# Seven products of quarters instead of eight in the first product of both swiglus

## The chip, the cores and the metric

The kernel runs on one core of a Trainium2 chip. Five compute engines with queues of their own work side by side: PE multiplies matrices into PSUM, ACT, DVE and POOL work on elements, SP starts transfers. The metric is the device time of one launch in microseconds (us). A profiled execution adds a trace; all times of single instructions below are from that one.

## The reference, cut to what matters

Two transformer blocks of D = 1024 are computed one after the other, all in fp32. The first has two layers over 512 latent tokens (and, in layer 0, 256 context tokens), each a mixer and then a swiglu of hidden width 2816:

```
def swiglu(h, w_in, w_out):
    gt, up = jnp.split(h @ w_in, 2, axis=-1)
    return (jax.nn.silu(gt) * up) @ w_out
...
hf = rms_norm(x, norm_ffn[l]) * (1.0 + sc_f) + sh_f
x = x + g_f * swiglu(hf, ffn_w_in[l], ffn_w_out[l])
```

In layer 0 the swiglu runs over 512 + 256 = 768 tokens, in layer 1 over 512. The second block (two layers, another kind of MLP) is not touched by the change.

## The kernel before, in words

Activations lie transposed: features on the 128 partitions, 8 slices k of 128 features, tokens along the free dimension (`XT` latent, `XC` context). An fp32 product is made of three faster ones: a factor is split into a rounded high part and the rest (`split`: a cast on ACT, a subtraction on DVE), and high x high, high x low and low x high are added up in PSUM (`product`, L273, L275, L277).

Weights come through the class `Weights`: SP loads a block of up to 2048 columns into a buffer `wst` (`WST` = 2 of them and the block in use), ACT casts it to `whi` (L91), DVE subtracts to `wlo` (L92), each with `WSP` = 2 buffers. So a block is split while the one before is multiplied, and its cast waits until PE has left the buffer two blocks back.

`swiglu` goes over the hidden width in 22 tiles of 128 rows. One tile (`up`) is one weight block of two products, gate and up (8 slices x 3 matmuls each, over 512 + 258 columns in layer 0 and 256 + 258 in layer 1; two columns carry the shift `sh_f`). DVE takes each from PSUM: L648 copies the shift columns, L649 multiplies by `rb`, the row of 1/rms; then ACT makes Silu (L651), DVE the product with the up part (L652), and `split` makes `uh` and `ul`. After 8, 7 and 7 tiles the second product (`down`) runs over what is there, in four steps of two output tiles, and adds its share to the residual (L450). The last part's `down` steps also feed the next norm.

The input of the first product is formed by `feed_mod(k)` as each slice k of the residual is finished: POOL adds its square to `acc` (L328, for the norm), ACT scales and casts it to `nmh` (L597), DVE makes `nml` (L598). The factor 1/rms is not known then; it is applied after the product, by `rb`, which is made within the first tile (`rstd`, L418, and `rbcast`, L343).

The program is written in steps; within an engine the order of instructions is set by a scheduler, each engine then runs its own queue in order and waits at its head. PSUM is handed out in four tiles of 1024 columns (`ps()`).

Of the kernel before, what the change touches and what calls it, by code (L numbers as in the profile page):

```python
# [23 lines left out]
WST = 2  # L24
WSP = 2
# [31 lines left out]
class Weights:  # L57
# [21 lines left out]
    def split(self, i):  # L79
        b = self.b  # L80
        nc = b.nc
        stage, n = self.loaded[i]
        self.loaded[i] = None
        desc, raw = self.desc[i]
        if raw:
# [3 lines left out]
        hi = b.wpool.tile([P, 2048], FR, tag="whi", name="whi", bufs=WSP)  # L89
        lo = b.wpool.tile([P, 2048], FR, tag="wlo", name="wlo", bufs=WSP)  # L90
# [29 lines left out]
class Builder:  # L120
# [158 lines left out]
    def pair(self, tiles, xh, xl, k0=0, kt=KT, outs=None, first=True, last=True):  # L279

        ps = self.ps() if outs is None else outs
        self.product(
            tiles, xh, xl, k0, kt, [(0, L)], [[ps[:, j * L : (j + 1) * L]] for j in range(len(tiles))], first, last
        )
        return ps

# [292 lines left out]
    def open_mod(self, l, side):  # L579


        n = L if l else T
        self.enter("nm", nm=(1, None, side))
        parts = [self.nm.tile([P, KT, n + 32], FR, name=m) for m in ("nmh", "nml")]
        self.feeds = parts + [self.nm.tile([P, n], F32, name="nmr"), self.nm.tile([P, KT, 4], F32, name="nmg")[:, :, 0:2]]
        self.gains(l, 1, self.feeds[3])
        self.split(self.M[:, l, 24:32, :], *(a[:, :, n : n + 2] for a in parts))

    def feed_mod(self, k, n):

        nc = self.nc
        hi, lo, _, G = self.feeds
        for z, (c0, m) in enumerate([(0, L)] + ([(L, C)] if n > L else [])):
            self.squares(k, c0, m, nc.gpsimd)
            g = G[:, k, z : z + 1]
            h = hi[:, k, c0 : c0 + m]
            nc.scalar.activation(h, self.x(k, c0, m), AF.Copy, scale=g)  # L597
            nc.vector.scalar_tensor_tensor(  # L598
                lo[:, k, c0 : c0 + m], self.x(k, c0, m), g, h.bitcast(F32), ALU.mult, ALU.subtract
            )  # L600


    def swiglu(self, l):
        wi, wo = self.I["ffn_w_in"][l], self.I["ffn_w_out"][l]
        n = T if l == 0 else L
        if l == 1:
            self.step(lambda: self.open_norm(("norm_mix_2", 0)))
        self.scope_step("ffn", hid=(1, None))

        if n == T:  # L610
            segs, at = [(0, L), (L, C + 2)], [(0, L), (L, T + 2)]
            tokens = lambda a: a[:, 0:T]
            runs = [(lambda a: a[:, 0:L], T), (lambda a: a[:, L:T], T + 1)]
        else:
            segs, at = [(0, C), (C, C + 2)], [(0, C), (L, L + C + 2)]
            tokens = lambda a: a.rearrange("p (s n) -> p s n", n=a.shape[1] // 2)[:, :, 0:C]
            runs = [(tokens, L + C)]

        def product(tile):
            o = self.ps()  # L620
            hi, lo, _, _ = self.feeds
            self.product([tile], hi, lo, 0, KT, segs, [[o[:, a:e] for a, e in at]])
            return o

        parts = [(0, 8), (8, 7), (15, 7)]
        for q, (t0, nt) in enumerate(parts):

            def alloc():
                self.uh = self.hid.tile([P, 8, n], FR, tag="uh", name="uh")
                self.ul = self.hid.tile([P, 8, n], FR, tag="ul", name="ul")  # L630

            self.step(alloc)
            for i in range(nt):

                def up(v, i=i, start=q == 0 and i == 0):
                    nc = self.nc
                    rb = self.feeds[2]
                    og = product(v[0])
                    if start:
                        self.rstd(n)  # L640
                    ou = product(v[1])
                    if start:
                        nc.scalar.copy(rb, self.rbcast(n)[:, 0:n])
                    s, u = self.t(n), self.t(n)
                    sh = self.tmp.tile([P, 2, 2], F32, tag="sh", name="sh")
                    c = runs[0][1]
                    for y, o, d in ((0, og, s), (1, ou, u)):
                        nc.vector.tensor_copy(sh[:, y], o[:, c : c + 2])  # L648
                        nc.vector.tensor_tensor(tokens(d), tokens(o), tokens(rb), ALU.mult)  # L649
                    for z, (run, _) in enumerate(runs):  # L650
                        nc.scalar.activation(run(s), run(s), AF.Silu, bias=sh[:, 0, z : z + 1])  # L651
                        nc.vector.scalar_tensor_tensor(run(s), run(u), sh[:, 1, z : z + 1], run(s), ALU.add, ALU.mult)  # L652
                    self.split(s, self.uh[:, i, :], self.ul[:, i, :])

                self.step(up, (blk(wi, 0, KT, (t0 + i) * P, P), blk(wi, 0, KT, FF + (t0 + i) * P, P)))
            for i in range(0, KT, 2):

                def down(v, i=i, q=q, nt=nt):
                    if n == T:
                        outs = self.full(cols(v), self.uh, self.ul, 0, nt)  # L660
                    else:
                        o = self.pair(cols(v), self.uh, self.ul, 0, nt)
                        outs = [o[:, 0:L], o[:, L : 2 * L]]
                    for j in range(2):
                        k = i + j
                        self.residual(outs[j][:, 0:L], k, 0, L, self.mod(l, 5, k, 0))
                        if n == T:
                            self.residual(outs[j][:, L:T], k, L, C, self.mod(l, 5, k, 1))
                        if q == 2:
                            if n == T:  # L670
                                self.squares(k, 0, L)
                                self.squares(k, L, C)
                            else:
                                self.feed(k)

                self.step(down, (blk(wo, t0, nt, i * P, 2 * P),))
        self.leave_step("ffn")
        self.leave_step("nm")
# [169 lines left out]
def even_mixer(b):  # L848
# [1491 lines left out]
```

## Time and the profile before

| | |
|---|---|
| median of 3 runs | 3628.89 us (3626.35 to 3630.6) |
| profiled execution, its time | 3626.45 us |
| its span (first to last instruction) | 3624.4 us |
| mean granted TensorE clock | 0.988 of full speed |
| busy: PE, DVE, ACT, POOL | 96%, 50%, 33%, 2% of the span |

The span is all but 2 us of the time. A busy share is an average over stages: what an engine can take on in one stage is read from that stage's rows. An instruction's time in a row runs from its start to its end, and neighbours overlap at their edges by some 0.08 us.

### The profile page before, as it was taken

To read this page: it belongs to the slowest core of one execution; us is meant where nothing else is said; L and a number is where in the kernel's file an instruction comes from. 1 tells how busy PE (TensorE), PEld (TensorE's weight loads), DVE (VectorE), ACT (ScalarE), POOL (GpSimd) and SP (SyncE) were. 2 spreads that over 40 slices of the span, in tenths; PEclk is the share of its full clock that TensorE was granted. 3 is DMA by queue.
4 is the path that set the end of the run, shared out by engine and by line. 5 is a ranking of instruction groups with operands and counts; after the bars stand their busy time and mean duration, and the time that the engine had idled before them with its cause. 6 is when DMAs were issued, how large, how long until landed. Compare 5 with 4: busy or idle time off the path is not lost.

```text
span 3624.4 us, 46788 instructions
## 1 busy us (share of the span) xinstructions
PE 3495.5 (96%) x19754; PEld 3013.2 (83%) x19754; DVE 1807.6 (50%) x3145; ACT 1187.7 (33%) x1810; POOL 72.0 (2%) x87
## 2 busy tenths in 40 slices
PE   6999899999999989999999999999999999999998
PEld 4767777888888879988999888888889999988886
DVE  5657555653233345565444555444554444454445
ACT  4356545432121233343222322222334234222222
POOL 0000000020000001001000000000000000000000
PEclk9999999999999999999999999999999999999999
DMA  6111455422222223222333233333232222233332
GB/s 232 48 57 65 147 165 190 138 59 70 59 64 59 66 85 82 74 63 82 94 89 100 85 88 106 98 99 93 87 102 77 83 71 76 75 95 93 93 98 71
DMA packets 351873, 333.17 MB, mean 92 GB/s; under 512 B 22192, under 2 KB 293296, under 8 KB 351664
## 3 DMA queue, kind: packets, MB, share of 16 engines
q1 hardware_dynamic: 330320, 313.88, 27.8%
q10 hardware_dynamic: 21344, 16.30, 1.5%
q8 instruction: 155, 2.54, 0.3%
q14 instruction: 54, 0.44, 0.0%
HBM read 312.62 MB, written 15.96 MB: 91 GB/s over the span
## 4 chain that ended last, share of the span: by engine, by line
PE 91%; DVE 4%; ACT 2%; DMA 1%; issue 1%; SPq 0%; POOL 0%; ACTq 0%; DVEq 0%
PE ps L277 19%; PE ps L275 19%; PE ps L273 19%; PE ps L310 5%; PE ps L312 5%; PE ps L311 5%; PE ps L1332 3%; PE ps L1704 1%; PE ps L1705 1%; PE ps L1706 1%; PE psc L1332 1%; PE ds L986 1%; PE pp L273 1%; PE pp L275 1%; PE pa L515 1%
## 5 line engine op out<-in xcount | busy, mean ns | idle before, releaser
L91 ACT CAST whi<-wst 128x2048 fp32r<-128x2048 f32 (+5 forms) x245 | 442.1, 1805 | 1281.5 <-PE ps L275 910.9
L92 DVE TENSOR_TENSOR wlo<-wst,whi 128x2048 fp32r<-128x2048 f32 (+5 forms) x245 | 529.8, 2162 | 157.3 <-ACT whi L91 150.2
L275 PE MATMUL ps<-ul,whi 128*128 128x512 f32 (+1 forms) x1040 | 361.9, 375 | 0.0
L277 PE MATMUL ps<-uh,wlo 128*128 128x512 f32 (+1 forms) x1040 | 361.4, 375 | 0.0
L273 PE MATMUL ps<-uh,whi 128*128 128x512 f32 (+1 forms) x1040 | 359.8, 374 | 0.0
L277 PE MATMUL ps<-nhh,wlo 128*128 128x512 f32 x864 | 340.1, 394 | 0.0
L275 PE MATMUL ps<-nhl,whi 128*128 128x512 f32 x864 | 338.0, 392 | 0.0
L273 PE MATMUL ps<-nhh,whi 128*128 128x512 f32 x864 | 337.0, 390 | 0.0
L275 PE MATMUL ps<-nml,whi 128*128 128x258 f32 (+2 forms) x1408 | 322.7, 310 | 2.3 <-DVE nml L598 2.0
L273 PE MATMUL ps<-nmh,whi 128*128 128x258 f32 (+2 forms) x1408 | 319.9, 309 | 4.2 <-ACT nmh L597 4.2
L277 PE MATMUL ps<-nmh,wlo 128*128 128x258 f32 (+2 forms) x1408 | 322.5, 310 | 0.6 <-DVE wlo L92 0.6
L310 PE MATMUL ps<-whi,nhh 128*128 128x512 f32 x576 | 238.0, 413 | 0.0
L273 PEld LDWEIGHTS ps<-nmh,whi 128*128 128x128 f32 x1408 | 216.8, 188 | 20.8 <-issue 4.6
L275 PEld LDWEIGHTS ps<-nml,whi 128*128 128x128 f32 x1408 | 216.4, 189 | 18.4 <-DVE nml L598 4.1
L277 PEld LDWEIGHTS ps<-nmh,wlo 128*128 128x128 f32 x1408 | 216.7, 189 | 16.2 <-DVE wlo L92 0.9
L311 PE MATMUL ps<-wlo,nhh 128*128 128x512 f32 x576 | 230.2, 400 | 0.0
L312 PE MATMUL ps<-whi,nhl 128*128 128x512 f32 x576 | 229.9, 399 | 0.0
L275 PEld LDWEIGHTS ps<-ul,whi 128*128 128x128 f32 x1040 | 184.1, 188 | 38.3
L273 PEld LDWEIGHTS ps<-uh,whi 128*128 128x128 f32 x1040 | 183.0, 188 | 36.6
L277 PEld LDWEIGHTS ps<-uh,wlo 128*128 128x128 f32 x1040 | 183.6, 188 | 35.5
L275 PEld LDWEIGHTS ps<-nhl,whi 128*128 128x128 f32 x864 | 162.2, 188 | 37.5
L273 PEld LDWEIGHTS ps<-nhh,whi 128*128 128x128 f32 x864 | 162.2, 188 | 35.4
(439 smaller groups left out, 6037.1 us busy)
## 6 DMA issues: line engine op xcount, KB each, us to landing
wst<-in_ffn_w_in_dram SPq DMA_DIRECT2D x88, 512.0 KB, 4.9
wst<-in_ada_w_dram SPq DMA_DIRECT2D x42, 1024.0 KB, 5.2
wst<-in_attn_w_qkv_dram SPq DMA_DIRECT2D x36, 1024.0 KB, 5.1
wst<-in_mlp_w_up_dram SPq DMA_DIRECT2D x32, 1024.0 KB, 5.5
wst<-in_mlp_w_down_dram SPq DMA_DIRECT2D x32, 1024.0 KB, 5.0
wst<-in_even_w_in_dram SPq DMA_DIRECT2D x14, 1024.0 KB, 5.3
wst<-in_ffn_w_out_dram SPq DMA_DIRECT2D x16, 896.0 KB, 4.6
wst<-in_odd_w_in_dram SPq DMA_DIRECT2D x12, 1024.0 KB, 5.2
```

The costliest lines, as they stand in the source:

```text
L91: nc.scalar.copy(hi[:, :n], stage[:, :n])
L92: nc.vector.tensor_tensor(lo[:, :n], stage[:, :n], hi.bitcast(F32)[:, :n], ALU.subtract)
L273: nc.tensor.matmul(outs[t][s], wh[:, k, :], xh[:, k0 + k, c0 : c0 + n], start=st, stop=False)
L275: nc.tensor.matmul(outs[t][s], wh[:, k, :], xl[:, k0 + k, c0 : c0 + n], start=False, stop=False)
L277: nc.tensor.matmul(outs[t][s], wl[:, k, :], xh[:, k0 + k, c0 : c0 + n], start=False, stop=sp)
L310: nc.tensor.matmul(o, lhs_h(4 * kk + k, 2 * i + j), wh[:, k, :], start=st, stop=False)
L311: nc.tensor.matmul(o, lhs_h(4 * kk + k, 2 * i + j), wl[:, k, :], start=False, stop=False)
L312: nc.tensor.matmul(o, lhs_l(4 * kk + k, 2 * i + j), wh[:, k, :], start=False, stop=sp)
L515: nc.tensor.matmul(ps[32 * k : 32 * k + 32, :], self.c2[:, a + 32 * k : a + 32 * k + 32], v[:, k, :], start=st, stop=sp,)
L986: nc.tensor.matmul(ps[:, o : o + w_], b.qkT[0][rows, h, j * P : (j + 1) * P], b.qkT[1][rows, h, c0 : c0 + w_], start=True, stop=True,)
L1332: mark = nc.tensor.matmul(out, lhsT, rhs, start=start, stop=stop)
L1704: nc.tensor.matmul(o, b.hh[:, k, at], wh[:, k, :], start=k == 0, stop=False)
```

## The change: what it does

The weight of a tile is a 2 x 2 matrix of quarters: rows gate (a11, a12) and up (a21, a22), columns the first and the last four slices k. The input is cut likewise: b11 and b12 are the two halves of the tokens for k < 4, b21 and b22 for k >= 4. The product of 2 x 2 quarters, eight products of quarters before, is made as seven (Strassen's algorithm in Winograd's form): P1 = a11 b11, P2 = a12 b21, P3 = s1 t1, P4 = s2 t2, P5 = s4 b22, P6 = s3 t3, P7 = a22 t4, where the s are sums of weight quarters and the t sums of input quarters. Each is 4 slices x 3 matmuls over 384 + 2 columns in layer 0 and 256 + 2 in layer 1: 84 matmuls for a tile.

`combine` forms the weight sums on POOL (L123 in the numbering of the changed kernel; ring `ws` of `WSUM` = 5), and splits in two groups, {a11, a12, s1, s2} and {s4, s3, a22}: six casts and six subtractions of 3584 columns in all, where there was one of each over 2048. Each group takes one `whi` and one `wlo` buffer. `quarters` runs the products in PSUM areas R, Q and V and takes them out between: ACT copies R or V to SBUF, DVE adds Q, V or R to the copies. The multiplication by `rb` is no longer part of the eviction: it follows on SBUF data, on DVE for gate and on POOL for up (L780).

`feed_mod` forms and splits b11, t1 (k < 4) and b21, b22, t2 (k >= 4) with each slice. `rest_mod` forms t3 (POOL) and t4 (DVE) within the first tile, after P3. `down` runs after 4, 4, 4, 4, 4 and 2 tiles, in two steps of four output tiles, so residuals are added six times. In the mixer of layer 0 the slices are fed in another order.

```diff
+        if raw == FAST:
+            self.done.append(self.combine(stage, desc))
...
+    def combine(self, stage, desc):
...
+            nc.gpsimd.tensor_tensor(s, a, b, op)
...
+        s1 = sum_(a21, a22, ALU.add)
+        s2 = sum_(s1, a11, ALU.subtract)
+        s4 = sum_(a12, s2, ALU.subtract)
+        s3 = sum_(a11, a21, ALU.subtract)
+        out = {}
+        for group in (((("a11", "a12"), v[:, 0]), (("s1",), s1), (("s2",), s2)), ((("s4",), s4), (("s3",), s3), (("a22",), a22))):
+            hi, lo = (t.rearrange("p (i k c) -> p i k c", i=4, c=P)[:, :, :q] for t in self.parts())
...
+                self.b.split(src, h, l)
...
+    def quarters(self, w, x, n, g, u, late=None):
...
+        add(R, "a11", "b11", True)
+        nc.scalar.copy(g[:, 0], R)
+        add(Q, "a12", "b21", True)
+        add(V, "s1", "t1", True)
+        nc.scalar.copy(u[:, 1], V)
+        nc.vector.tensor_tensor(g[:, 0], g[:, 0], Q, ALU.add)
+        if late is not None:
+            late()
+        add(R, "s2", "t2", False)
+        nc.scalar.copy(g[:, 1], R)
+        add(V, "s4", "b22", False)
+        nc.vector.tensor_tensor(g[:, 1], g[:, 1], V, ALU.add)
+        add(R, "s3", "t3", False)
+        nc.scalar.copy(u[:, 0], R)
+        nc.vector.tensor_tensor(u[:, 1], u[:, 1], R, ALU.add)
+        add(Q, "a22", "t4", True)
+        nc.vector.tensor_tensor(u[:, 0], u[:, 0], Q, ALU.add)
...
+            nc.vector.tensor_tensor(t2, t2h, t2l, ALU.add)
+            nc.gpsimd.tensor_tensor(t3, t2, b11h, ALU.subtract)
+            nc.gpsimd.tensor_tensor(t3, t3, b11l, ALU.subtract)
+            nc.vector.tensor_tensor(t4, b21h, t2, ALU.subtract)
+            nc.vector.tensor_tensor(t4, t4, b21l, ALU.add)
+            self.factor("t3", k, t3)
+            self.factor("t4", k, t4)
...
-        parts = [(0, 8), (8, 7), (15, 7)]
+        parts = [(t0, min(4, FF // P - t0)) for t0 in range(0, FF // P, 4)]
...
+                    for d, eng in ((s, nc.vector), (u, nc.gpsimd)):
+                        eng.tensor_tensor(d[:, :, 0:m], d[:, :, 0:m], rb, ALU.mult)
```

How the queues change is shown at three places of layer 1. On ACT, two tiles in the middle of the first part of 8 stood like this before (L651 Silu, L91 the next block's cast, L242 `uh`):

```order
L651 ACTIVATE t_15115<-t_15115,sh_15117 128x512 [waits DVE_49]
L91 CAST whi_15129<-wst_15008 128x2048 [waits DMAHW1_49,DMAHW2_49,PE_49,Activation_49]
L242 CAST uh_15015<-t_15115 128x512 [waits DVE_49]
L651 ACTIVATE t_15231<-t_15231,sh_15233 128x512 [waits DVE_49]
L91 CAST whi_15245<-wst_15126 128x2048 [waits DMAHW3_49,DMAHW4_49,PE_49,Activation_49]
L242 CAST uh_15015<-t_15231 128x512 [waits DVE_49]
```

In the changed kernel one tile in the middle of a part has these rows (t_16605 and t_16606 are the gate and up buffers of this tile, t_16474 the gate buffer of the tile before, whi_16589 the first group of the tile after; L348, L351, L356 and L360 are the copies after P1, P3, P4 and P6):

```order
L348 COPY t_16605<-ps_16607 128x258 [waits PE_49]
L283 CAST uh_16472<-t_16474 128x512 [waits DVE_49]
L351 COPY t_16606<-ps_16608 128x258 [waits PE_49]
L283 CAST whi_16589<-wst_16445 128x1024 [waits DMAHW3_49,PE_49,Activation_49]
L283 CAST whi_16589<-ws_16581 128x512 [waits Pool_49]
L283 CAST whi_16589<-ws_16583 128x512 [waits Pool_49]
L356 COPY t_16605<-ps_16607 128x258 [waits PE_49]
L360 COPY t_16606<-ps_16607 128x258 [waits PE_49]
L784 ACTIVATE t_16605<-t_16605 128x256 [waits DVE_49]
L784 ACTIVATE t_16605<-t_16605 128x256
L283 CAST whi_16597<-ws_16585 128x512 [waits PE_49,Activation_49,Pool_49]
```

ACT now holds copies that PE waits for, and the copy after P4 stands behind three casts for the next tile; the cast of `uh` stands between the copies of the next tile.

On POOL nothing stood there before. Now, at the same place (wst_16445 is the block of the third tile of the part, wst_16578 that of the fourth; t_16475 and t_16606 are the up buffers of the first and the second):

```order
L123 TENSOR_TENSOR ws_16581<-wst_16445 128x512 [waits DMAHW4_49,DVE_49]
L123 TENSOR_TENSOR ws_16583<-ws_16581,wst_16445 128x512 [waits DMAHW3_49,DVE_49,Pool_49]
L123 TENSOR_TENSOR ws_16585<-wst_16445,ws_16583 128x512 [waits DVE_49,Pool_49]
L780 TENSOR_TENSOR t_16475<-t_16475,nmr_14256 128x2x256 [waits DVE_49]
L123 TENSOR_TENSOR ws_16587<-wst_16445 128x512 [waits DVE_49]
L123 TENSOR_TENSOR ws_16711<-wst_16578 128x512 [waits DMAHW6_49,DVE_49]
L123 TENSOR_TENSOR ws_16713<-ws_16711,wst_16578 128x512 [waits DMAHW5_49,DVE_49,Pool_49]
L123 TENSOR_TENSOR ws_16715<-wst_16578,ws_16713 128x512 [waits DVE_49,Pool_49]
L780 TENSOR_TENSOR t_16606<-t_16606,nmr_14256 128x2x256 [waits DVE_49]
```

The multiplication that a tile's up half waits for stands behind three weight sums of a tile two further on.

On DVE, where layer 1's first tile begins, these rows stood before (L450 the last residuals of the mixer, L598 the last three `nml`):

```order
L450 SCALAR_TENSOR_TENSOR XT_70<-ps_13784,M_90,XT_70 128x512 [waits PE_49]
L450 SCALAR_TENSOR_TENSOR XT_70<-ps_13784,M_90,XT_70 128x512
L92 TENSOR_TENSOR wlo_13813<-wst_13692,whi_13812 128x2048 [waits DMAHW4_49,DMAHW3_49,Activation_49]
L598 SCALAR_TENSOR_TENSOR nml_13704<-XT_70,nmg_13706,nmh_13703 128x512 [waits DVE_49,Activation_49] x3
L648 COPY sh_13959<-ps_13835 128x2 [waits PE_49]
```

Now 27 rows stand between the last residual and the last low part of t3; the last of them (L716 the low parts of b21 and b22, L737, L740 and L741 the sums for t3 and t4, ps_14479 an area of the first tile, wlo_14429 the low part of the second tile's first group):

```order
L716 SCALAR_TENSOR_TENSOR b21l_14251<-XT_70,nmg_14257,b21h_14250 128x256 [waits Activation_49]
L716 SCALAR_TENSOR_TENSOR b22l_14253<-XT_70,nmg_14257,b22h_14252 128x256 [waits Activation_49]
L284 TENSOR_TENSOR t2l_14255<-t_14413,t2h_14254 128x256 [waits Activation_49]
L737 TENSOR_TENSOR scr_14472<-t2h_14254,t2l_14255 128x256 x2
L740 TENSOR_TENSOR scr_14472<-b21h_14250,scr_14472 128x256 [waits DVE_49] x2
...
L352 TENSOR_TENSOR t_14476<-t_14476,ps_14479 128x258 [waits Activation_49]
...
L284 TENSOR_TENSOR wlo_14429<-wst_14215,whi_14428 128x1024 [waits DMAHW3_49,PE_49,Activation_49]
L284 TENSOR_TENSOR wlo_14429<-ws_14420,whi_14428 128x512 [waits Activation_49]
L284 TENSOR_TENSOR wlo_14429<-ws_14422,whi_14428 128x512 [waits Activation_49]
L284 TENSOR_TENSOR t4l_14464<-scr_14472,t4h_14463 128x256 [waits Activation_49]
L284 TENSOR_TENSOR t3l_14462<-scr_14473,t3h_14461 128x256 [waits Activation_49]
```

The last low part of t3 stands behind a weight group whose cast waits for the end of P4 of the same tile.

## Rows read from the trace of the kernel before

**Rows 1.** The page: busy time by engine, and the chain that ended last.
```profile
PE 3495.5 (96%) x19754; PEld 3013.2 (83%) x19754; DVE 1807.6 (50%) x3145; ACT 1187.7 (33%) x1810; POOL 72.0 (2%) x87
...
PE 91%; DVE 4%; ACT 2%; DMA 1%; issue 1%; SPq 0%; POOL 0%; ACTq 0%; DVEq 0%
```

**Rows 2.** Timeline, DVE, layer 0's swiglu: start, us, instruction, idle before and its releaser.
```profile
1004.04 0.16 DVE L648 COPY sh<-ps 128x2 f32<-128x2 f32 x1 [3.05 <-PE ps L277]
...
1020.84 0.16 DVE L648 COPY sh<-ps 128x2 f32<-128x2 f32 x1 [3.05 <-PE ps L277]
```

**Rows 3.** Timeline, DVE, layer 1's swiglu.
```profile
1833.24 0.16 DVE L648 COPY sh<-ps 128x2 f32<-128x2 f32 x1 [4.91 <-PE ps L277]
...
1844.58 0.16 DVE L648 COPY sh<-ps 128x2 f32<-128x2 f32 x1 [4.91 <-PE ps L277]
```

**Rows 4.** Groups of ACT by line and shape: count | busy us, mean ns | idle before.
```profile
L242 ACT CAST uh<-t 128x512 fp32r<-128x512 f32 x22 | 13.7, 622 | 2.7 <-DVE t L652 2.1
L91 ACT CAST whi<-wst 128x1024 fp32r<-128x1024 f32 x9 | 9.5, 1053 | 44.1 <-PE ps L275 38.4 <-issue 5.6
L1506 ACT COPY vv<-ps 128x384 f32<-128x384 f32 x32 | 15.2, 478 | 18.1 <-PE ps L1332 17.8
L1112 ACT COPY XC<-pp 128x256 f32<-128x256 f32 x12 | 4.4, 370 | 4.4 <-PE pp L277 4.4
```

**Rows 5.** Groups of DVE by line and shape.
```profile
L243 DVE TENSOR_TENSOR ul<-t,uh 128x768 fp32r<-128x768 f32 x22 | 20.9, 951 | 0.9 <-ACT uh L242 0.9
L652 DVE SCALAR_TENSOR_TENSOR t<-t,sh 128x512 f32<-128x512 f32 x44 | 33.1, 752 | 4.5
L598 DVE SCALAR_TENSOR_TENSOR nml<-XT,nmg,nmh 128x512 fp32r<-128x512 f32 x16 | 18.4, 1163 | 0.9 <-ACT nmh L597 0.9
L243 DVE TENSOR_TENSOR ul<-t,uh 128x512 fp32r<-128x512 f32 x22 | 15.1, 684 | 0.1
L92 DVE TENSOR_TENSOR wlo<-wst,whi 128x1024 fp32r<-128x1024 f32 x9 | 11.0, 1223 | 2.7 <-ACT whi L91 2.2
L328 DVE TENSOR_TENSOR acc<-acc,t 128x256 f32<-128x256 f32 x16 | 6.8, 423 | 8.3 <-ACT t L327 7.7
```

**Rows 6.** Groups of POOL by line and shape.
```profile
L328 POOL TENSOR_TENSOR acc<-acc,t 128x512 f32<-128x512 f32 x14 | 24.5, 1751 | 548.2 <-PE ps L277 365.2 <-ACT t L327 182.7
L1689 POOL TENSOR_TENSOR B<-al,fconsts 128x512 f32<-128x512 f32 x12 | 15.8, 1346 | 120.5 <-DVE z L1782 58.1 <-DVE z L1779 36.6 <-DMA al<-in_rpbr_dram 16.9
L376 POOL TENSOR_TENSOR hl<-t,hh 128x768 fp32r<-128x768 f32 x8 | 14.7, 1834 | 579.9 <-PE pa L515 561.8 <-DVE t L374 18.1
```

**Rows 7.** Timeline, POOL, where layer 1's swiglu begins.
```profile
1681.93 6.26 POOL L328 TENSOR_TENSOR acc<-acc,t 128x512 f32<-128x512 f32 x3 [1.58 <-ACT t L327]
```

**Rows 8.** Timeline, DVE, the same place.
```profile
1682.15 3.21 DVE L92 TENSOR_TENSOR wlo<-wst,whi 128x2048 fp32r<-128x2048 f32 x1
1685.28 4.12 DVE L598 SCALAR_TENSOR_TENSOR nml<-XT,nmg,nmh 128x512 fp32r<-128x512 f32 x3
```

**Rows 9.** Timeline, PE, the same place: the mixer's end, the first and the second tile's start.
```profile
1677.97 0.40 PE L277 MATMUL ps<-hh,wlo 128*128 128x512 f32 x1
1682.54 0.48 PE L273 MATMUL ps<-nmh,whi 128*128 128x256 f32 x2 [4.17 <-ACT nmh L597]
...
1697.46 0.48 PE L273 MATMUL ps<-nmh,whi 128*128 128x256 f32 x2
```

**Rows 10.** Windows of PE, the same place: length, busy (count), granted clock, DMA share, GB/s.
```profile
1683.00:1684.00 1.00, 1.00 (x7) 0.50 0.00 0
...
1685.00:1686.00 1.00, 1.00 (x6) 0.50 0.00 0
1686.00:1687.00 1.00, 1.00 (x10) 0.86 0.23 63
1687.00:1689.00 2.00, 2.00 (x17) 1.00 1.03 299
```

**Rows 11.** Timeline, PE, layer 0's start: fourth slice's product nearly done, second tile's start.
```profile
755.69 0.51 PE L277 MATMUL ps<-yl,wlo 128*128 128x512 f32 x2
...
796.88 0.53 PE L273 MATMUL ps<-nmh,whi 128*128 128x512 f32 x2
```

More of the change, by code (lines that the diff above doesn't have):

```diff
@@ L24 @@
 WST = 2
+WSUM = 5
+FAST = "fast"
 WSP = 2
@@ L285, in pair, with add @@
         return ps
+    def quarters(self, w, x, n, g, u, late=None):
+        nc = self.nc
+        one, two = self.ps(), self.ps()
+        R, Q, V = one[:, 0:n], two[:, 0:n], two[:, L : L + n]
+        def add(o, a, b, first):
+            (wh, wl), (xh, xl) = w[a], x[b]
+            kt = wh.shape[1]
+            for k in range(kt):
+                for i, (c, d) in enumerate(((wh, xh), (wh, xl), (wl, xh))):
+                    nc.tensor.matmul(
+                        o, c[:, k], d[:, k, :n], start=first and k + i == 0, stop=k == kt - 1 and i == 2,
+                        skip_group_check=not first,
+                    )
+        add(R, "a11", "b11", True)
[15 more added lines that the diff above has]
+        nc.vector.tensor_tensor(u[:, 0], u[:, 0], Q, ALU.add)
     def full(self, tiles, xh, xl, k0=0, kt=KT, first=True, last=True):
@@ L579, in open_mod @@
     def open_mod(self, l, side):
+        nc = self.nc
         n = L if l else T
+        m = self.half = n // 2
+        self.side = side
         self.enter("nm", nm=(1, None, side))
[L584 to L587, printed above, removed]
+        self.fx = {}
@@ new lines, in open_mod, with factors, shifts @@
+        self.shifts((("b11", sh[:, 0:4]), ("t1", self.zero[:, 0]), ("b21", sh[:, 4:8]), ("b22", sh[:, 4:8]), ("t2", sh[:, 4:8])))
+        kw = {"bufs": 6} if l else {}
+        self.first_t = [self.yp.tile([P, n], F32, name="y", **kw) for _ in range(2)]
+    def factors(self, pool, names):
+        for x in names:
+            self.fx[x] = [pool.tile([P, 4, self.half + 8], FR, name=x + p)[:, :, : self.half + 2] for p in "hl"]
+    def shifts(self, what):
+        for name, src in what:
+            self.split(src, *(a[:, :, self.half :] for a in self.fx[name]))
@@ L644, in up @@
[L644 to L652, printed above, removed]
@@ L653, in up @@
-                    self.split(s, self.uh[:, i, :], self.ul[:, i, :])
-                self.step(up, (blk(wi, 0, KT, (t0 + i) * P, P), blk(wi, 0, KT, FF + (t0 + i) * P, P)))
-            for i in range(0, KT, 2):
-                def down(v, i=i, q=q, nt=nt):
[L659 to L666, printed above, removed]
-                        if n == T:
-                            self.residual(outs[j][:, L:T], k, L, C, self.mod(l, 5, k, 1))
-                        if q == 2:
-                            if n == T:
[L671 to L676, printed above, removed]
+                        nc.scalar.copy(self.rb, self.rbcast(n)[:, 0:n])
@@ L1295, in last @@
             b.feed_mod(k, T)
+            if k == 3:
+                for i in range(4, 7):
+                    add(b.full([tiles[i]], *b.yl, 0, 1)[0], i)
+                    b.feed_mod(i, T)
     b.leave_step("gc")
```

159 lines of the change are left out of this document (126 added, 33 removed).

## The prediction

> **What bounds the kernel now.** I read the page first: PE is busy 96% of the span and makes 91% of the chain that ended last [rows 1]. Then the stage of the change, by DVE's timeline, since DVE takes the products out of PSUM as they end. In layer 0 the copies of gate's shift columns come 1020.84 - 1004.04 = 16.80 us apart, each after DVE has waited for PE [rows 2]; in layer 1 1844.58 - 1833.24 = 11.34 [rows 3]. So both swiglus run at PE's pace, and DVE waits several us in each tile. A tile is 48 pairs of matmuls (2 products x 8 slices x 3): .350 us for 512 + 258 columns, .236 for 256 + 258, so .118 for some 257 columns and .232 for 512. ACT and DVE look idle at 33% and 50%, POOL all but unused at 2%; that is over the span, and the change asks all three for more in stages that will be shorter.
>
> **1. PE's work.** 84 matmuls for a tile. With 258 columns, a little over .118, say .1185: x 84 = 9.95 us. With 386 columns, between the two known lengths: .118 + (386 - 257)/(512 - 257) x (.232 - .118) = .176, x 84 = 14.76 us. Saved: 22 x (16.80 - 14.76) = 44.9 and 22 x (11.34 - 9.95) = 30.5, together **-75** (2% of the time). `down` keeps its matmuls. Its residuals are doubled (six parts for three), on DVE under PE's products. Transfers are the same. Everything below is what is paid out of these 75.
>
> **2. A copy behind three casts.** P6 adds on to R, so it waits until ACT has copied R after P4. In ACT's new order that copy stands behind the three casts of the next tile's first group, and these wait for the end of P4 themselves, since P4 is the last to read the buffer that they fill. From the end of P4: casts of 1024, 512 and 512 columns, 1.05 + .62 + .62 [rows 4], less .08 of overlap each, 2.05; then the copy, .48 for 384 columns or .37 for 256 [rows 4], and some .1 to PE: 2.6 and 2.5 us. Meanwhile PE has only P5: 12 x .176 = 2.11 or 12 x .1185 = 1.42. PE waits .5 a tile in layer 0 and 1.1 in layer 1: 22 x (.5 + 1.1) = **+36**. I see nothing that could hide it: there is no other matmul in PE's queue between P5 and P6. The bounds are 30 and 42 (a tenth of a us either way on the hand-over).
>
> **3. DVE against POOL.** Before, nothing ran on POOL in these stages. What happens when both work is to be seen where layer 1's swiglu begins: during POOL's three additions, 6.26 us [rows 7], DVE's subtraction of 2048 columns took 3.21, and its three `nml` 4.12 together, 1.37 each [rows 8], as against .75 for an instruction of that kind and size elsewhere (L652 [rows 5]). Two such operations of 512 columns take some 1.7 to 2 us a pair, about the sum of the two alone: they take turns. An addition of 512 on POOL is then some 1.2 to 1.3 of its own (1.35 in the quieter group, 1.75 as a mean in the disturbed one [rows 6]).
> The Trainium skill, "SBUF — State Buffer", section "SBUF: two separate sides", says the same: the port pair that DVE and GpSimd share is an exclusive lock for the whole instruction when the DVE operation has two SBUF inputs and GpSimd's reads SBUF. It speaks against this change, which puts five such POOL instructions into each tile beside six subtractions on DVE that now hold more columns; by it the upper bound below is the value, and the sum 12 us higher.
> Per tile in layer 1: POOL 5 x 1.2 = 6.0 (four sums and the multiplication of `up`); DVE's operations with two SBUF inputs: subtractions of 3584 columns, 1.22 + 4 x .68 less overlaps, about 4.2 (1024 + five of 512, one of them in a pair: 3.5 times the 1024 row), multiplication .61, the product .7, `ul` .6 [rows 5]: 6.1. Taking turns throughout, 12.1 to 12.4 us against the 9.95 + 1.1 of steps 1 and 2: 1.1 to 1.3 over, 22 x 1.25 = 27. In layer 0: POOL 4 x 1.2 + 1.8 (768 columns [rows 6]), DVE 4.2 + .9 + 1.1 + .9: 13.7, under 15.3. There only the order can cost: the multiplication of `up` stands behind three weight sums of a later tile, the Silu product, the cast of `uh` and the next tile's copy after P3 behind it. Bounds: 0 (all turns fall into DVE's idle time) and 27 + 3 = 30. Between them I take **+18**, nearer to the upper one, since [rows 7, 8] show no turn that was free, but `down` between the parts gives DVE and POOL time to catch up.
>
> **4. The two starts.** In layer 1, PE's last product of the mixer ends at 1678.4, the first tile starts at 1682.5 and ends at 1697.46 [rows 9]. With 9.95 for 11.34 it should end at 1696. Now P2 waits for all b21, P6 for t3, P7 for t4. Of DVE's queue 27 rows stand between the last residual and t3's last low part, 24 of some 256 columns and a weight group: 24 x .42 [rows 5] + 2.6 = 12.7 us; from 1679.5 that is 1692, and P6's end and P7 after it 1695: free of cost if nothing disturbs it. POOL in that time has four squares, 4 x 1.3, eight instructions for t3 of about half that, and one to two sums: some 12 us; with turns throughout the tile ends at 1707. Excess 0 to 13; I take 10, because t3 goes from DVE to POOL, ACT and back to DVE, four times, and the last low part also stands behind the weight group whose cast waits for P4. In layer 0 it is 41.2 us from the fourth slice's product to the second tile [rows 11], 39.2 with PE's saving. The same queues, with 384 columns and two segments, give by the same walk 43 to 57; the excess is 4 to 18, I take 12. After the wait of 4.17 us [rows 9] the granted clock was .50 for over three us [rows 10], that is 1.2 instead of 2.4 GHz, and cost 1.7 us (half of the 3 us shown at .50, and .14) and a little more at the edges; one more such wait in each first tile adds 2 each, +4. Sum **+26**, bounds 4 and 37.
>
> **5. Parts.** Six part switches for three. For the last part of 2 tiles `down` begins with one slice for four output tiles (12 products: 4.2 or 2.8 us), while the second tile's eviction still wants an addition, POOL's multiplication (1.3), Silu, product and cast, four to five us. Some 1 to 2 us for each such place, and about .5 for each further switch: **+5**, bounds 0 and 10.
>
> **The sum**: -75 + 36 + 18 + 26 + 5 = +10 against the profiled 3626.45 us: 3636. That execution was 2.4 us below the median, so against the median of 3628.89 I say **3638**.
>
> **The rivals.**
> A, the forecast: what PE saves is paid back, a little more than all of it. Its own range is 3618 to 3658.
> B, faster: the second engine's turns are mostly free (step 3: 3) and the starts cost a third (9), while the copy still stands behind its casts: -75 + 36 + 3 + 9 + 3 = -24, **3605**. For it: DVE waits 4.9 us at a time in layer 1's tiles now [rows 3], so room exists. Against it: 6.0 + 6.1 us of turns fill an 11 us tile. It decides at step 3: as soon as a tile of layer 1 holds 11.34 us, half of the gain is gone.
> C, clearly slower: turns everywhere (+30), full starts (+37), parts +10: -75 + 36 + 30 + 37 + 10 = +38, **3667**. For it: [rows 7, 8].
> D, PE-bound throughout: only step 1 counts; the starts at their lower bound: **3558**. For it: PE's 96% and DVE's idle time [rows 1, 2]. Against it: ACT's order of the copy, which does not depend on how fast anything is.
> E, the clock: if PE's short waits, three to five in each tile, take the granted clock down as the one of 4.17 us did [rows 9, 10], then once in each tile, at 1.9 us, is 44 x 1.9 = 84 on top of A: **3720**, and 3680 for layer 1 alone. The Trainium skill, "TensorE: Matmul & The Clock Gate", section "HAM oscillation — how this bites in real kernels", warns of such a pattern of bursts and waits. No stage of this trace has one to show it.
>
> **How the numbers follow.** Chances: A .42, B .27, C .18, D .08, E .05. A difference of 0.2%, some 7 us, is about what a measurement of this kernel can tell from none. Faster: D and B, and the tenth of A below 3622: .39. Same, 3622 to 3636: a good third of A, .15. Slower: the rest of A, C and E: .46. For the range I leave out most of D, E and the far end of C: 3575 to 3675, which holds B and A whole.
>
> **What the profile of the changed kernel would show.** Step 1: a tile's products at 84 x .176 and .1185 where PE doesn't wait, and matmul groups of 386 and 258 columns. Step 2: in every tile a wait of PE before P6, released by ACT's copy (L356), some .5 and 1.1 us; if P6 starts straight after P5, step 2 is wrong, and 36 us with it. Step 3: POOL's sums at 1.7 us and more as a mean instead of 1.2 to 1.35, DVE's subtractions of 512 well over .7, tiles of layer 1 at 12.3 us; if these tiles last 11 us, B is right. Step 4: the first tile of layer 1 ends some 10 us after 1696 counted from the mixer's end, with the granted clock at half in stretches of it. Wrong would be the whole if the turns cost DVE only for a fraction of an instruction, or if weight sums on POOL last much longer than additions did before, so that POOL's queue itself, five instructions in a tile, becomes the pace.

## The result, and the profile after

The changed kernel takes 3688.72 us in the median (3679.65 to 3690.28, 4 runs) against 3629.74 of the kernel before (4 runs): a ratio of 1.0158, 95% interval 1.0140 to 1.0177. It is slower by 59 us, where the forecast said 9, and it lies outside the range. Its profiled execution took 3679.65 us, the shortest of its four runs and 53.2 more than that of before; its span is 3677.9. What follows accounts for these 53. The page of the changed kernel:

```profile
PE 3459.5 (94%) x19226; PEld 3016.2 (82%) x19226; DVE 2150.6 (58%) x3625; ACT 1355.8 (37%) x2306; POOL 442.1 (12%) x323
...
PE 82%; DVE 10%; ACT 4%; issue 2%; DMA 1%; POOL 0%; ACTq 0%; DVEq 0%; SPq 0%
```

PE is busy 36 us less than in [rows 1], but the chain that ended last holds 10% of DVE instead of 4%. DVE is busy 343 us longer. Where the time went is read from the first matmul of each part of the swiglus, in PE's timeline. Before, where a part of 7 tiles begins and the next one (layer 0 first, layer 1 below; 767.04 is the first of all, 1332.21 nearly the last matmul of layer 0):

```profile
767.04 0.39 PE L273 MATMUL ps<-nmh,whi 128*128 128x512 f32 x1
...
978.63 0.39 PE L273 MATMUL ps<-nmh,whi 128*128 128x512 f32 x1
...
1155.60 0.39 PE L273 MATMUL ps<-nmh,whi 128*128 128x512 f32 x1
...
1332.21 0.51 PE L277 MATMUL ps<-uh,wlo 128*128 128x512 f32 x2
...
1821.70 0.28 PE L273 MATMUL ps<-nmh,whi 128*128 128x256 f32 x1
...
1940.24 0.28 PE L273 MATMUL ps<-nmh,whi 128*128 128x256 f32 x1
```

After, where a part of 4 tiles begins and the next one:

```profile
780.49 0.36 PE L342 MATMUL ps<-b11h,whi 128*128 128x386 f32 x1
...
902.34 0.34 PE L342 MATMUL ps<-b11h,whi 128*128 128x386 f32 x1
...
998.48 0.34 PE L342 MATMUL ps<-b11h,whi 128*128 128x386 f32 x1
...
1334.95 0.52 PE L318 MATMUL ps<-uh,wlo 128*128 128x512 f32 x2
...
1698.03 0.55 PE L342 MATMUL ps<-b11h,whi 128*128 128x258 f32 x1 [12.03 <-ACT b22h L715]
...
1785.44 0.28 PE L342 MATMUL ps<-b11h,whi 128*128 128x258 f32 x1
...
1860.09 0.28 PE L342 MATMUL ps<-b11h,whi 128*128 128x258 f32 x1
```

Four tiles with their share of `down` took 4/7 x (1155.60 - 978.63) = 101.1 us in layer 0 and 4/7 x 118.54 = 67.7 in layer 1. Now they take 96.1 and 74.7; the four full parts of layer 1 after the first last 74.65, 74.8, 72.3 and 74.8, 74.1 in the mean. So layer 0's tiles gain 22/4 x 5.0 = 27 us, and layer 1's lose 22/4 x 6.4 = 35. The rest is at the starts. Layer 0's first tile begins 780.49 - 767.04 = 13.4 us later, and its first part lasts 121.8, 25.7 more than a later one, where before the first of 8 tiles had 211.6 - 8 x 25.3 = 9.3 too much: 16.4 more. From the end of layer 0's swiglu to layer 1's first tile it is 363.1 us for 350.3 [rows 9]: 12.8 more. Layer 1's first part is 87.4, 13.3 over the mean of the later ones, against 139.2 - 8 x 16.9 = 3.7 before: 9.6 more. That makes 52 for the two starts. What is left, some -6, lies in the last short parts and in the program behind (3.5 us shorter).

**One tile of layer 1.** The columns are start, duration, instruction, idle time before it with its releaser. PE, the second tile of a part: the product after P4, and the granted clock around it (length, busy, clock, DMA share, GB/s):

```profile
1805.82 0.58 PE L342 MATMUL ps<-b22h,whi 128*128 128x258 f32 x1 [3.74 <-DVE t L352]
```

```profile
1801.00:1804.00 3.00, 1.08 (x9) 1.00 0.00 0
...
1806.00:1807.00 1.00, 1.00 (x5) 0.50 1.14 345
...
1810.00:1811.00 1.00, 1.00 (x7) 0.50 0.00 0
1811.00:1813.00 2.00, 2.00 (x17) 0.88 0.00 0
```

DVE, POOL and ACT in the same stretch, one fence each:

```profile
1798.40 3.18 DVE L284 TENSOR_TENSOR wlo<-ws,whi 128x512 fp32r<-128x512 f32 x2 [0.82 <-ACT whi L283]
1801.51 1.76 DVE L284 TENSOR_TENSOR wlo<-wst,whi 128x512 fp32r<-128x512 f32 x1
1803.19 0.87 DVE L785 SCALAR_TENSOR_TENSOR t<-t 128x256 f32<-128x256 f32 x2
1804.74 0.69 DVE L284 TENSOR_TENSOR ul<-t,uh 128x512 fp32r<-128x512 f32 x1 [0.68 <-ACT uh L283]
1805.35 0.42 DVE L352 TENSOR_TENSOR t<-t,ps 128x258 f32<-128x258 f32 x1
```

```profile
1799.39 1.64 POOL L780 TENSOR_TENSOR t<-t,nmr 128x512 f32<-128x512 f32 x1
1801.00 1.72 POOL L123 TENSOR_TENSOR ws<-wst 128x512 f32<-128x512 f32 x1
```

```profile
1804.09 0.62 ACT L283 CAST uh<-t 128x512 fp32r<-128x512 f32 x1 [4.41 <-DVE t L785]
1804.62 0.37 ACT L351 COPY t<-ps 128x258 f32<-128x258 f32 x1
1804.88 1.05 ACT L283 CAST whi<-wst 128x1024 fp32r<-128x1024 f32 x1
1805.83 1.14 ACT L283 CAST whi<-ws 128x512 fp32r<-128x512 f32 x2
1806.87 0.37 ACT L356 COPY t<-ps 128x258 f32<-128x258 f32 x1
```

Read from the end of the chain back: P5 waits for L352, the addition of Q; that stands behind `ul` on DVE, `ul` behind the cast of `uh` on ACT, the cast behind the Silu product (L785), and that behind DVE's subtractions of the second weight group, which take 1.6 to 1.76 us each instead of .68 [rows 5], one after each of POOL's instructions. The clock stands at 1.2 GHz (.50) for five us after the wait, which costs another 2.5 (half of the five). The copy after P4 (L356) stands behind its three casts as forecast, but PE had still P5 and some of the next tile's matmuls to do: after layer 1's first tile (.3 us there) PE waits for L356 nowhere. What PE waits before P5 in the four full parts of layer 1 after the first (us, times, longest), and its clock over them:

```profile
PE ps L342 <- DVE t L352: 27.7, 12, 3.8
```

```profile
1785.00:2082.00 297.00, 267.89 (x1732) 0.94 0.29 86
```

**Layer 1's start.** PE's last product of the mixer, then DVE's last residual behind the sum for a factor (L720):

```profile
1685.61 0.39 PE L318 MATMUL ps<-hh,wlo 128*128 128x512 f32 x1
```

```profile
1696.59 0.47 DVE L720 SCALAR_TENSOR_TENSOR t<-XT,nmg,y 128x256 f32<-128x256 f32 x1
1696.98 0.73 DVE L528 SCALAR_TENSOR_TENSOR XT<-ps,M,XT 128x512 f32<-128x512 f32 x1
```

The residual ends at 1697.71 and P1 begins .3 us later. The trace names an instruction of ACT (b22h, L715) as releaser; that P1 waited for the residual, which frees its PSUM area, is inferred from this and from e11, where the residuals come earlier and P1 with them. PE stood still for 12.0 us, where it was 4.2 before [rows 9].

### The profile page after: what moved, and what is told of

Same layout as the page of the kernel before. It is cut to its first block, busy times and chain, and to the rows that moved or that the text cites. A ratio compares the mean times of both kernels' runs of the same rounds, so it can differ in the third digit from the quotient of the medians.

```text
span 3677.9 us, 47155 instructions
## 1 busy us (share of the span) xinstructions
PE 3459.5 (94%) x19226; PEld 3016.2 (82%) x19226; DVE 2150.6 (58%) x3625; ACT 1355.8 (37%) x2306; POOL 442.1 (12%) x323
## 4 chain that ended last, share of the span: by engine, by line
PE 82%; DVE 10%; ACT 4%; issue 2%; DMA 1%; POOL 0%; ACTq 0%; DVEq 0%; SPq 0%
PE ps L318 13%; PE ps L314 13%; PE ps L316 13%; PE ps L342 11%; PE ps L388 5%; PE ps L390 4%; PE ps L389 4%; PE ps L1492 3%; DVE wlo L284 3%; PE ps L1864 1%; PE ps L1865 1%; PE ps L1866 1%; PE psc L1492 1%; PE ds L1142 1%; PE pp L314 1%
## 5 line engine op out<-in xcount | busy, mean ns | idle before, releaser
L96 ACT CAST whi<-wst 128x2048 fp32r<-128x2048 f32 (+5 forms) x201 | 358.2, 1783 | 819.8 <-PE ps L316 608.2
L97 DVE TENSOR_TENSOR wlo<-wst,whi 128x2048 fp32r<-128x2048 f32 (+5 forms) x201 | 434.3, 2160 | 163.9 <-ACT whi L96 161.6
L123 POOL TENSOR_TENSOR ws<-wst 128x512 f32<-128x512 f32 x88 | 152.8, 1736 | 760.6 <-DMA wst<-in_ffn_w_in_dram 610.3
L318 PEld LDWEIGHTS ps<-nhh,wlo 128*128 128x128 f32 x864 | 162.9, 189 | 37.7 <-DVE wlo L97 2.5
L526 DVE TENSOR_TENSOR XT<-ps,XT 128x512 f32<-128x512 f32 x80 | 51.5, 686 | 236.3 <-PE ps L318 236.3
L528 DVE SCALAR_TENSOR_TENSOR XT<-ps,M,XT 128x512 f32<-128x512 f32 x126 | 91.8, 747 | 143.0 <-PE ps L318 142.9
L284 DVE TENSOR_TENSOR wlo<-ws,whi 128x512 fp32r<-128x512 f32 x176 | 161.1, 956 | 6.3 <-ACT whi L283 6.3
L389 PEld LDWEIGHTS ps<-wlo,nhh 128*128 128x128 f32 x576 | 156.0, 271 | 7.2
```

The source lines that it names most:

```text
L123: nc.gpsimd.tensor_tensor(s, a, b, op)
L284: self.nc.vector.tensor_tensor(lo, src, hi.bitcast(F32), ALU.subtract)
L318: nc.tensor.matmul(outs[t][s], wl[:, k, :], xh[:, k0 + k, c0 : c0 + n], start=False, stop=sp)
L389: nc.tensor.matmul(o, lhs_h(4 * kk + k, 2 * i + j), wl[:, k, :], start=False, stop=False)
```

## The experiments

All are edits of the changed kernel; ratios are to the kernel before, with 95% intervals. "Four tiles" is read as above, in layer 0 and in layer 1.

**e1: no sums.**
```diff
-            s = self.b.wpool.tile([P, 4, P], F32, tag="ws", name="ws", bufs=WSUM)[:, :q]
-            nc.gpsimd.tensor_tensor(s, a, b, op)
-            return s
+            return a
```


> The four weight sums of a tile are left out: quarters stand in their place (the products are then not those of the reference); everything else stays. Theory (chain): in layer 1's tiles PE waits before P5 because DVE's subtractions of the next tile's second group take turns with POOL's sums (1.7 us each instead of some .65), and the Silu product, the cast of uh, its low part and the addition after P2 (L352) come late one behind the other; the clock falls after these waits. Without sums the waits before P5 fall from 36 us to under 8, a tile of layer 1 from 13 to some 10.5 us, clock 1.00 there: 3615 to 3640 us. Rival (step 2 of the forecast, a copy behind three casts): the waits need no POOL, so a wait before P6 of .5 and 1.1 us a tile appears: not under 3655 us.


3637.25 us, 1.0020 (1.0010 to 1.0030): 51 us less. Four tiles 94.5 and 67.0. PE's waits and its clock in layer 1's full parts after the first, in e1 (L350 is the addition of Q):
```profile
PE ps L340 <- DVE t L350: 12.4, 12, 1.0
```
```profile
1776.00:2044.00 268.00, 254.16 (x1731) 1.00 0.32 95
```
The time is the theory's, the waits are not quite: without POOL's sums they halve (27.7 to 12.4), where the theory had them under a quarter, but none is over 1.0 us and the clock stays up. The order of the instructions of the chain is that of the changed kernel in every tile. No wait before P6 appears.

**e2: the copy after P4 on DVE.**
```diff
-        nc.scalar.copy(g[:, 1], R)
+        nc.vector.tensor_copy(g[:, 1], R)
```


> The copy of R after P4 is made by DVE, so that it no longer stands behind ACT's three casts. Rival (step 2): up to 36 us less, 3650 to 3665. Theory (chain): the copy is not what PE waits for, and DVE has one instruction more in each tile: 3680 to 3705, with the waits before P5 unchanged or longer.


3665.3 us, 1.0097 (1.0082 to 1.0112): 23 less, at the upper end of the rival's range; the theory's number missed. But the trace shows another reason than the rival's: the scheduler now placed two other instructions differently. ACT in e2, one tile:
```profile
1871.10 0.38 ACT L351 COPY t<-ps 128x258 f32<-128x258 f32 x1 [0.40 <-PE ps L342]
1875.10 0.62 ACT L283 CAST uh<-t 128x512 fp32r<-128x512 f32 x1 [3.62 <-DVE t L785]
```
The copy of V now stands ahead of the cast of the last tile's `uh`, and on DVE L352 ahead of `ul`, so two links of the chain are gone: the waits before P5 are 20.9 us in the four full parts, 27.7 in the changed kernel, and still DVE's. The edit did not isolate what it was to isolate.

**e3: the multiplication of up on DVE.**
```diff
-                    for d, eng in ((s, nc.vector), (u, nc.gpsimd)):
+                    for d, eng in ((s, nc.vector), (u, nc.vector)):
```


> The multiplication of up by rb moves from POOL to DVE. Theory (chain): the Silu product no longer waits for an instruction that stands behind three weight sums, but the subtractions in front of it still take turns: some of the 36 us before P5 go, 3660 to 3685. Rival (only the sum of the turns counts, 12.2 us in a tile of layer 1): 6.0 + 6.1 becomes 4.8 + 6.7, .7 us a tile, 3670 to 3680, and the waits before P5 shrink in all tiles alike. Rival (step 2): no change, 3680 to 3695.


3657.07 us, 1.0080 (1.0063 to 1.0097). Four tiles 95.8 and 69.9; the waits before P5 fall to 15.6, the longest to 2.4 us, and the clock is back at .99. That is 32 us less, more than either theory said. But the scheduler placed the copy of V ahead of `uh` and L352 ahead of `ul` here too, as in e2, so the 32 us are not those of one POOL instruction alone.

**e4: V in a PSUM tile of its own.**
```diff
-        one, two = self.ps(), self.ps()
-        R, Q, V = one[:, 0:n], two[:, 0:n], two[:, L : L + n]
+        one, two, three = self.ps(), self.ps(), self.ps()
+        R, Q, V = one[:, 0:n], two[:, 0:n], three[:, 0:n]
```


> V gets a PSUM tile of its own instead of the second half of Q's. Theory (chain): P5 writes V and waits for DVE's addition that reads Q only because both lie in one PSUM tile; with two tiles it waits for ACT's copy of V, which ended .8 us before that addition in the trace: 22 x .8 = 18 us less and some clock with it, 3655 to 3675. Rival (the addition is not what holds P5 up, the cast of uh in front of both is, and PSUM areas turn over faster): 3680 to 3700. Rival (step 2): no change.


3653.08 us, 1.0064 (1.0049 to 1.0079). Four tiles 94.5 and 69.6. PE's waits in layer 1's tiles in e4:
```profile
PE ps L342 <- ACT t L351: 17.3, 8, 4.1
```
P5 had waited for L352 only because Q and V shared a PSUM tile; now it waits for ACT's copy, which is late for the same reason: it stands behind the cast of `uh`. It is 36 us less, 2 more than the theory's range allows; L352 stands ahead of `ul` in this run, which may be part of it.

**e5: two factors instead of seven.**
```diff
-            for o, x, c in two:
-                e = o + x.shape[1]
-                nc.vector.scalar_tensor_tensor(f[:, o:e], x, c, b[:, o:e], ALU.mult, ALU.subtract)
-            self.factor("t1", k, f)
...
-        for name, parts in (("b21", [(0, one, g[0])]), ("b22", two)):
+        for name, parts in (("b21", [(0, one, g[0])]),):
...
-        self.factor("t2", k, t)
...
-                    self.quarters(v, self.fx, m + 2, s, u, self.rest_mod if start else None)
+                    x = self.fx
+                    x = {"b11": x["b11"], "b21": x["b21"], "t1": x["b11"], "t2": x["b21"], "b22": x["b21"], "t3": x["b11"], "t4": x["b21"]}
+                    self.quarters(v, x, m + 2, s, u, None)
```


> Only b11 and b21 are formed and split; they stand for t1, t3 and for b22, t2, t4, so the products are not those of the reference, but all 84 matmuls of a tile and all weight sums stay. That leaves DVE less to do for the input than in the kernel before. Theory: the two starts cost 52 us more than before by the trace (residuals that free PSUM stand in DVE's queue behind the factors, then t3 and t4), and most of that goes: 3638 to 3655. Rival (the starts cost the 26 of the forecast, the rest of the loss is in the tiles): 3660 to 3668.


3644.4 us, 1.0045 (1.0028 to 1.0062): 44 less. Four tiles are unchanged, 95.8 and 74.3. Reckoned as above, the starts cost 18 us in place of 52: 34 of them go with the factors.

**e6: the split of uh behind the next tile's copy.** The edits of e3 and e4, and:
```diff
         nc.vector.tensor_tensor(g[:, 0], g[:, 0], Q, ALU.add)
+        if self.held is not None:
+            self.held()
+            self.held = None
...
-                    self.split(s[:, :, 0:m], h, l)
+                    if i == nt - 1:
+                        self.split(s[:, :, 0:m], h, l)
+                    else:
+                        self.held = lambda: self.split(s[:, :, 0:m], h, l)
```


> Three edits together: V in a PSUM tile of its own, the multiplication of up on DVE, and the split of uh and ul issued after the next tile's copy and addition that follow P3 (the scheduler now places the cast of uh behind the copy of V on ACT). POOL keeps the four sums. Theory (chain): P5 waits for nothing of the tile before any more; four tiles of layer 1 with their share of down fall from 74.7 us to some 64 to 66, the clock stays at 1.00: 3630 to 3645. Rival (the turns between POOL and DVE fill the tile, the order hardly matters): 68 to 70 us for four tiles as in the single edits, 3645 to 3655.


3649.18 us, 1.0054 (1.0039 to 1.0069): the rival's number. Four tiles 94.5 and 68.7. The waits before P5 are all but gone, and in their place PE waits before P6, in layer 1's tiles of e6 (L359 is the copy after P4):
```profile
PE ps L342 <- ACT t L359: 14.0, 8, 2.5
PE ps L342 <- DVE t L352: 0.6, 1, 0.6
```
So the order alone does not mend it. With P5 on time, the copy behind three casts, step 2 of the forecast, is the next in line.

**e7: as e6, the sums on DVE too.**
```diff
-            nc.gpsimd.tensor_tensor(s, a, b, op)
+            nc.vector.tensor_tensor(s, a, b, op)
```


> As e6_uh_behind_copy, and the four weight sums on DVE too, so that nothing runs on POOL in the tiles. Theory (turns): no instruction waits for the other engine, but DVE has 11 us of work of its own in a tile of layer 1 against 10.1 on PE: 66 to 68 us for four tiles, 3625 to 3650. Rival (POOL's turns cost nothing once the order is mended): slower than e6 by 5 us and more, as DVE only has more to do.


3621.27 us, 0.9982 (0.9972 to 0.9991): 28 us under e6, and below the theory's own range. Four tiles 94.5 and 64.0, at a clock of 1.00. PE and then DVE in e7:
```profile
1768.00:1832.00 64.00, 63.36 (x433) 1.00 0.33 99
```
```profile
1844.53 0.68 DVE L284 TENSOR_TENSOR wlo<-wst,whi 128x512 fp32r<-128x512 f32 x1
1845.14 1.28 DVE L784 TENSOR_TENSOR t<-t,nmr 128x512 f32<-128x512 f32 x2
1846.34 0.68 DVE L123 TENSOR_TENSOR ws<-ws,wst 128x512 f32<-128x512 f32 x1
```
Each instruction of 512 columns takes .68 again, and PE is busy 63.4 of 64 us. In layer 1 the scheduler put six to eight matmuls between P5 and P6, most of them of P7, which cover the copy. So e7 changes the order as well as the engine of the sums.

**e8: as e6, in layer 0 alone.** Layer 1's swiglu and its input are those of the kernel before.
```diff
     def swiglu(self, l):
+        if l:
+            return self.old_swiglu(l)
```


> The edits of e6, with seven products in layer 0 alone; layer 1's swiglu, its input and its parts are those of the kernel before. By the trace layer 0's tiles with their share of down gain 28 us, some 7 more with the edits, and its start loses 30: 3618 to 3632, if the stages are independent of each other. If layer 1 is slower for another reason than its own seven products, more than 3640.


3624.7 us, 0.9989 (0.9980 to 0.9998). Four tiles of layer 0 take 94.1. Layer 1's swiglu is as before to .1 us, so seven products in layer 0 do not slow it; its loss in the changed kernel is its own.

**e9: the sums on DVE, nothing else.** The edit of e7 alone.


> One edit on the changed kernel: the four weight sums of a tile on DVE instead of POOL; the order of the Silu product, uh and the copies stays, as does the multiplication of up on POOL. Theory (turns between POOL and DVE are what makes the chain late): DVE has 2.6 us more to do in a tile and is still earlier; four tiles of layer 1 from 74.7 to 66 to 69 us, clock near 1.00: 3635 to 3652. Rival (the order of the instructions is what counts, as e6 mended it without touching the sums): DVE's extra work delays the chain further, 3680 to 3700.


3648.68 us, 1.0053 (1.0039 to 1.0066): 40 less, though DVE has 176 instructions more. Four tiles 95.0 and 67.8. PE's waits and clock in layer 1's tiles of e9:
```profile
PE ps L342 <- DVE t L352: 13.4, 12, 1.6
```
```profile
1782.00:2054.00 272.00, 255.81 (x1735) 1.00 0.32 94
```
The scheduler changed the chain's order in the third tile of each part, so the tiles to compare are the second ones, where it is as it was. P5 there, in e9:
```profile
1800.44 0.39 PE L342 MATMUL ps<-b22h,whi 128*128 128x258 f32 x1 [1.59 <-DVE t L352]
```
It waited 3.7 to 3.8 us there in the changed kernel. Together with e1, which keeps the order everywhere and has 1.0, that decides between turns and order: POOL's sums make up the larger part of that wait. What is left, 1.0 us in the fourth tile as before, goes only with the order (e6).

**e10: as e7, the squares of feed_mod and t3 on DVE too.**
```diff
-            self.squares(k, c0, w, nc.gpsimd)
+            self.squares(k, c0, w)
...
-            nc.gpsimd.tensor_tensor(t3, t2, b11h, ALU.subtract)
-            nc.gpsimd.tensor_tensor(t3, t3, b11l, ALU.subtract)
+            nc.vector.tensor_tensor(t3, t2, b11h, ALU.subtract)
+            nc.vector.tensor_tensor(t3, t3, b11l, ALU.subtract)
```


> As e7_no_pool, and in the two starts the squares of feed_mod and the two subtractions for t3 on DVE too. Theory (an instruction of POOL keeps DVE out for its whole length, 1.3 us for 512 columns, while DVE does the same in .69): the starts lose some of their 48 us, 3606 to 3618. Rival (the starts are bound by DVE's own work): no gain or a loss, 3620 to 3630.


3610.86 us, 0.9946 (0.9933 to 0.9960), the best of all: 19 us under the kernel before and 78 under the changed one. The page of e10:
```profile
PE 3445.1 (95%) x19226; PEld 2999.9 (83%) x19226; DVE 2150.3 (60%) x3882; ACT 1360.4 (38%) x2306; POOL 40.6 (1%) x66
```
POOL gave up 402 us of work and 257 instructions to DVE, and DVE is busy for 2150.3 us where it was 2150.6: what it now computes it had spent before within longer instructions. Reckoned as above, the starts cost 45 us here and 54 in e7, so POOL had some 9 of them.

**e11: residuals first.** The changed kernel; in both mixers all residuals are issued before the first feed_mod, in layer 1 so:
```diff
             for j in range(2):
                 b.residual(o[:, j * L : (j + 1) * L], i + j, 0, L, b.mod(1, 2, i + j, 0))
-                b.feed_mod(i + j, L)
+        for k in range(KT):
+            b.feed_mod(k, L)
```


> On the changed kernel, one edit: where the two mixers end, all residuals are issued before the first feed_mod, so that they stand ahead of the factors in DVE's queue (the PSUM areas that the mixer's last products and P1 wait for come free by them). Theory (residuals behind factors are what PE waits for at the starts: 9.1 + 2.3 us in layer 0, 12.0 + 1.9 in layer 1): 15 to 25 us less, 3660 to 3675. Rival (DVE's whole work for the factors is what binds, the wait only moves to P2 or t3): 3680 to 3692.


3680.44 us, 1.0137 (1.0123 to 1.0150): 8 less, on the rival's side. The changed kernel's own runs lie 11 us apart, and the two profiled executions are alike (3679.43 and 3679.65 us), so a gain is not shown; reckoned as above, the starts still cost 52. P1 of layer 1 starts at 1691.22, 6.8 us earlier, but then PE waits for b21 and t3. PE in e11:
```profile
1698.93 0.58 PE L342 MATMUL ps<-b21l,whi 128*128 128x258 f32 x1 [2.92 <-DVE b21l L716]
...
1716.13 0.58 PE L342 MATMUL ps<-t3h,whi 128*128 128x258 f32 x1 [4.92 <-ACT t3h L283]
```

**e12: e10 with residuals first.** Both edits together.


> As e10_no_pool_at_all, with all residuals ahead of the factors in both layers. Theory (as in e11): 5 to 15 us less than e10, 3595 to 3606. Rival (DVE's work for the factors binds): within 4 us of e10, 3606 to 3615.


3611.23 us, 0.9946 (0.9933 to 0.9960): no gain over e10. With e5 and e11: the starts are bound by the amount of work for the factors, not by its order.

## Why the prediction was wrong

The forecast was +10 us on the profiled execution, and +53 was measured. Two terms carry the miss. In layer 1's tiles steps 1, 2, 3 and 5 came to +12, and 35 were paid: step 3 had the turns, but not the chain by which they reach P5, nor the clock that falls with the waits. Step 4 put 26 on the starts, and 52 were paid.

**Step 1, PE's work,** was right in kind and somewhat too large. Where almost nothing waits (e7), four tiles gain 101.1 - 94.5 and 67.7 - 64.0, over 22 tiles 36 + 20 = 57 us with the additional part switches, where steps 1 and 5 together said 70. A matmul of 258 columns comes every .12 us (P1 to P5 of a tile start 1.44 apart), not .1185, and one of 386 every .178 (2.14 apart), not .176.

**Step 2, the copy behind three casts,** failed as it was put. Its order was there, but the sentence that nothing stood in PE's queue between P5 and P6 was false: in the changed kernel's trace up to five matmuls of the next tile stand there in layer 1 and two in layer 0, and P5 itself was late. Its 36 us were not paid there. e6 shows the wait behind it, 14 us, once P5 is on time, and e7 shows it covered by another order.

**Step 3, the turns,** had the right mechanism, too small a size and the wrong path. DVE's subtractions of the second group took 1.6 to 1.76 us for .68, and a tile of layer 1 12.9 us ((74.1 - 22.4 for `down`) / 4) where the forecast's sign for turns throughout was 12.3. What was missed is the place where it bites: not the sum of the turns over a tile, but the chain from those subtractions over the Silu product, `uh` and `ul` to the addition that P5 waits for. P5 was tied to that addition by a PSUM tile shared by Q and V (e4). The waits before P5 are 27.7 us in four full parts. In e10 DVE took over 402 us of POOL's work and was busy no longer than before. The Trainium skill, "SBUF — State Buffer", section "SBUF: two separate sides", calls the pair of ports that the two engines share an exclusive lock, held for a whole instruction; these 2150.6 and 2150.3 us agree with it.

**The clock** was a rival of its own (E, .05) and came in part: .94 over those parts, where it was 1.00 in e1, e7 and e9. Of the 74.7 us of four tiles, PE's matmuls alone take 4 x 84 x .12 + 22.4 for `down` (4/7 x 118.54 - 4 x 11.34) = 62.7. About 6 to 7 of the other 12 are waits (27.7 over four parts), and about 4 the clock (6% of 67 us busy). The forecast gave it nothing beyond the starts.

**Layer 0's tiles** came out near the forecast, -45 + 11 + 2 + 2 = -30, measured -27, but by luck. PE's saving was some 7 us smaller (36 in e7 against 45 - 2), and the waits and the clock together cost 9 (36 - 27) where steps 2 and 3 had 13; what PE waited for stood before P5 and not before P6.

**Step 4, the starts,** said 26, and 52 were paid: a term mis-sized by half. The walk began at the last residual's usual time, as if nothing stood ahead of it. In the trace the residuals themselves are late: they stand in DVE's queue behind the factors, with POOL's squares between (9.1 us of PE before a product of layer 0, 12.0 in layer 1). e11 and e12 show that another order gains nothing, and e5 that the work for the factors is the larger part: 34 of the 52 go with it. The clock was mis-sized too, 4 us for both starts. PE over layer 1's first tile and the start of the second:
```profile
1698.00:1730.00 32.00, 22.09 (x110) 0.67 0.08 25
```
At .12 us each, these 110 matmuls would have taken 13.2 us: by this estimate the clock cost some 9 us here alone.

**The rivals.** C, turns throughout, priced at 3667, was nearest in kind, though it too counted step 2's 36 us, which were not paid there; what came was C's turns and starts, larger than priced, with part of E on top. E's 3680 for layer 1 alone is nearer by its number, but it put 42 us of clock into these tiles, where some 22 were lost (4 us in four tiles, by the estimate above). B and D needed POOL's turns to be free.

What stays open is the last third of the starts' cost, the 18 us that e5 still pays, and how the clock and the waits divide there: the 9 us are an estimate, and no run separates them.

## What to carry to other kernels

An idle engine is not a free one: where POOL and DVE work on the same stage, take the sum of both as DVE's load, as it came out here, and try the work on DVE itself first. In a queue that runs in order, follow the chain from the longest instruction to the next thing that PE waits for, and look at which matmuls the scheduler has left between; an average load of an engine says little. A saving of 2% of PE's work that needs seven factors at once instead of one is paid for at each start, and is worth the more the longer the stage behind it.

## What was not expected of the hardware

Giving 402 us of POOL's work to DVE left DVE's busy time as it was (2150.6 and 2150.3 us, e10, with the edits of e6); by the sums alone (e9) POOL lost 283 us and DVE gained 16. The granted clock fell to .50 after waits of PE shorter than the 4.17 us of [rows 9]: for five us after one of 3.74, and in e2 after one of 2.95 us, here with the windows of PE around it:

```profile
1875.45 0.39 PE L342 MATMUL ps<-b22h,whi 128*128 128x258 f32 x1 [2.95 <-DVE t L352]
```

```profile
1874.00:1876.00 2.00, 0.55 (x4) 0.98 0.13 34
1876.00:1877.00 1.00, 1.00 (x7) 0.50 0.98 285
...
1878.00:1879.00 1.00, 1.00 (x7) 0.50 1.19 295
```

In e9, where no wait in these tiles was longer than 1.6 us, it stayed at 1.00.
